# Latent attention's queries and keys made feature-major directly, with the rotation left to the score product

## The chip, the cores and the metric

The kernel runs on one core of one Trainium2 chip. The metric is the device time of one execution in microseconds (us); the number of a kernel is the median of its runs.

## The reference, cut to what matters

The model is a four-part encoder trunk (mixer, MLP, mixer, MLP) over 256 tokens of width 1024. The first mixer has two groups of heads side by side: eight heads of neighbourhood attention, and eight heads of latent attention, which the change touches. In these, queries come out of a normed latent of 256 features and keys and values out of a normed latent of 128; a query or key has 64 plain features and 32 that are rotated by position, and the 32 rotated key features are one vector shared by all heads.

```python
def apply_rope(x, cos, sin):
    ...
    x1, x2 = x[..., :half], x[..., half:]
    return jnp.concatenate([x1 * c - x2 * s, x2 * c + x1 * s], axis=-1)

def even_mixer(xn, w_in, rpb, q_norm, w_uq, kv_norm, w_ukv, w_o, cos_r, sin_r):
    hcat = xn @ w_in
    ...
    c_q = rms_norm(hcat[..., o0:o1], q_norm)
    c_kv = rms_norm(hcat[..., o1:o2], kv_norm)
    k_pe = apply_rope(hcat[..., o2:][:, :, None, :], cos_r, sin_r)
    q = (c_q @ w_uq).reshape(b, s, MLA_HEADS, MLA_NOPE + MLA_ROPE)
    q = jnp.concatenate([q[..., :MLA_NOPE], apply_rope(q[..., MLA_NOPE:], cos_r, sin_r)], axis=-1)
    kv = (c_kv @ w_ukv).reshape(b, s, MLA_HEADS, MLA_NOPE + MLA_V)
    k = jnp.concatenate([kv[..., :MLA_NOPE],
                         jnp.broadcast_to(k_pe, (b, s, MLA_HEADS, MLA_ROPE))], axis=-1)
    v = kv[..., MLA_NOPE:]
    out_b = dense_attention(q, k, v, (MLA_NOPE + MLA_ROPE) ** -0.5)
    return jnp.concatenate([out_a, out_b], axis=-1) @ w_o
```

## The kernel before

The program has four stages in a row: the even mixer, an MLP, the odd mixer, an MLP. Weights are read from HBM in pieces of up to 128 x 2048, four raw buffers deep, over SP's queue; each piece is split on ScalarE and VectorE into a high and a low fp32r half (`split`: a cast on ScalarE, line 175, and the remainder on VectorE, line 176; tiles `whi`, `wlo`), and a product is three matmuls, high by high, low by high and high by low (`mm3`, lines 179 to 181). The weights come in the order of a list (`plan`), and each call of `weight()` splits up to two pieces ahead.

In the even mixer the latents come first: `c_product` gives 416 columns a token (256 for queries, 128 for keys and values, 32 rotary), and `c_tail` (lines 511 to 531) norms them, rotates the 32 columns with four VectorE operations (`rope`, lines 494 to 498) into `kpe`, and hands back a step that turns the normed latent `cn` feature-major by three TensorE transposes (line 530) and splits it into `c`. There is one such step for each half `t` of the tokens; the two stand among the matmuls of the neighbourhood queries and keys. The first fills the time of `t` = 0 and the second that of `t` = 1.

Then `main` is a list of steps with costs in us, written by hand: the neighbourhood products, the latent queries (`uq_steps`) and keys and values (`ukv_steps`), and the output product (`out_steps`). `side` is the list of attention steps: for each n of 0 to 15, `scores(n)` (line 676; 0 to 7 neighbourhood, 8 to 15 latent, two heads and 128 tokens each), `turn_probs(n)` (transposes of the probabilities `pp`, line 709, copied to `pts`) and `mix` (line 724). A loop gives out as many side steps as the costs of the main steps have earned. The tile scheduler then fixes the order on each engine; an engine works through its queue strictly in that order.

A latent product is token-major: for each half `t` and four heads `h`, six matmuls of 384 columns give queries, ScalarE copies the plain features to `qtok`, VectorE rotates the others into it, and a later step `turn` makes four transposes of 128 x 96 (`heads_transposed`, line 615) and splits the outcome into `mq`. Keys and values are made together, three matmuls of 512 columns; ScalarE copies the keys to `ktok`, GpSimd copies `kpe` beside them (line 656), VectorE copies the values to `vml`, and four transposes and a split give `mk`. The scores contract over 96 features.

Of the kernel before, what the change touches and what calls it, by code (L numbers as in the profile page):

```python
# [23 lines left out]
P = 128  # L24
# [20 lines left out]
def trunk(ctx, tc, a, out):  # L45
# [37 lines left out]
    warm = const.tile([P, 512], mybir.dt.bfloat16, name="warm")  # L83
    nc.vector.memset(warm, 0.0)
    idle = bank("acc")
# [38 lines left out]
    plan("w_uq", 2 * 768)  # L124
# [346 lines left out]
    def even(ep):  # L471
# [30 lines left out]
        cT_h, cT_l = halves(quarter_pair("c"))  # L502
        kpe = ep.tile([P, NT, 32], F32, name="kpe")
# [7 lines left out]
        def c_tail(t, pc):  # L511
            rt = column(r, t)
            cn = scratch([384], "cn")
# [98 lines left out]
        def heads_transposed(n, t, h, src):  # L612
            pt = bank("w")
            for i in range(4):
                nc.tensor.transpose(pt[0:96, i * P:(i + 1) * P], src[:, i, :], ident)
            hs = slice(4 * h, 4 * h + 4)
            split(*(mT[n][0:96, hs, v, tok(t)] for v in range(2)), pt[0:96].rearrange("p (i n) -> p i n", i=4))

        def uq_steps():
            hold, src = {}, {}  # L620

            def gemm(t, h):
                if not hold:
                    hold["w"] = weight()
                    mT["q"] = pair_tile(ep, KT, "mq", 1, "mq")
                wh, wl = hold["w"]
                pq = bank("acc")
                for k in range(2):
                    ws = slice(k * 768 + h * 384, k * 768 + h * 384 + 384)
                    mm3(pq[:, 0:384], cT_h[:, k, tok(t)], cT_l[:, k, tok(t)], wh[:, ws], wl[:, ws], k == 0, k == 1)  # L630
                pq4 = pq[:, 0:384].rearrange("p (h d) -> p h d", d=96)
                s = src[t, h] = scratch([4, 96], "qtok")
                nc.scalar.copy(s[:, :, 0:64], pq4[:, :, 0:64])
                rope(s[:, :, 64:96], pq4[:, :, 64:96], 4, cosr[:, t, :], sinr[:, t, :], 16)

            def turn(t, h):
                heads_transposed("q", t, h, src.pop((t, h)))

            th = [(t, h) for t in range(NT) for h in range(2)]
            return [lambda v=v: gemm(*v) for v in th], [lambda v=v: turn(*v) for v in th]  # L640

        def ukv_steps():
            hold, src = {}, {}

            def gemm(t, h):
                if not hold:
                    hold["w"] = weight()
                    mT["k"] = pair_tile(ep, KT, "mk", 1, "mk")
                wh, wl = hold["w"]
                pk = bank("acc")  # L650
                ws = slice(h * 512, h * 512 + 512)
                mm3(pk, cT_h[:, 2, tok(t)], cT_l[:, 2, tok(t)], wh[:, ws], wl[:, ws], True, True)
                pk4 = pk.rearrange("p (h d) -> p h d", d=128)
                s = src[t, h] = scratch([4, 96], "ktok")
                nc.scalar.copy(s[:, :, 0:64], pk4[:, :, 0:64])
                nc.gpsimd.tensor_copy(s[:, :, 64:96], kpe[:, t, :].unsqueeze(1).broadcast_to([P, 4, 32]))
                nc.vector.tensor_copy(vml[:, t, h * 256:(h + 1) * 256].rearrange("p (h d) -> p h d", d=64), pk4[:, :, 64:128])

            def turn(t, h):
                heads_transposed("k", t, h, src.pop((t, h)))  # L660

            th = [(t, h) for t in range(NT) for h in range(2)]
            return [lambda v=v: gemm(*v) for v in th], [lambda v=v: turn(*v) for v in th]
# [12 lines left out]
        def scores(n):  # L676
# [7 lines left out]
            else:  # L684
                for j in range(2):
                    h = 2 * hp + j
                    q, k = (halves(mT[n][0:96, h]) for n in "qk")
# [55 lines left out]
        (ug, ut), (kg, kt) = uq_steps(), ukv_steps()  # L743
# [236 lines left out]
def _constants():  # L980
    con = {}
    con["cos_r"], con["sin_r"] = _tables(32, ORDER)
    con["cos_f"], con["sin_f"] = (np.ascontiguousarray(np.tile(z.transpose(1, 0, 2).reshape(T, HD).T, (2, 1)))
# [66 lines left out]
```

## Time and profile before

| | |
|---|---|
| median of 3 runs | 751.15 us (751.09 to 751.2) |
| the profiled execution | 751.89 us, of which 750.0 us span |
| PE (TensorE matmul) busy | 739.8 us, 99% |
| VectorE (DVE), ScalarE (ACT), GpSimd (POOL) busy | 542.3, 468.6, 9.5 us |
| share of TensorE in the chain that ended last | 93% |
| mean granted TensorE clock | 0.998 |

The span is the time from the first to the last instruction. The chain that ended last is followed back from the last instruction, at each step to what released it. A busy PE counts matmuls from their start to a modelled end, and neighbours overlap: the price of a matmul in a dense stretch is the distance between two starts, not the duration of one.

### The profile page before, as it was taken

The page shows a single profiled execution, that of the slowest core. Times are in us where ns is not written, and L with a number is a line of the kernel's source. Part 1 is how long each engine was busy: PE and PEld are TensorE (multiplying, and loading weights), DVE is VectorE, ACT ScalarE, POOL GpSimd, SP SyncE. Part 2 cuts the span into 40 slices and gives each one's busy share as a digit, 9 for nine tenths or more (in the row PEclk, how much of TensorE's full clock was granted, in tenths as well). Part 3 has the DMA queues.
Part 4 walks back from the last instruction along what each step waited for, and adds up shares of the span by engine and source line. Part 5 has one row for each costly group of instructions (what it writes and reads, how often), then busy time and mean ns, then how long its engine had stood idle before and what let it go on. Part 6 is the DMA issues. An engine that isn't in the chain of part 4 may idle for free.

```text
span 750.0 us, 12208 instructions
## 1 busy us (share of the span) xinstructions
PE 739.8 (99%) x4572; PEld 644.8 (86%) x4572; DVE 542.3 (72%) x1143; ACT 468.6 (62%) x1059; POOL 9.5 (1%) x22
## 2 busy tenths in 40 slices
PE   8999999999999999999999999999999999999996
PEld 5887899888888888989899898998998888888885
DVE  6798859766656656998877787877759665666664
ACT  6688887545545446857785866867757554554541
POOL 0100000000000000000000000000000000000000
PEclk9999999999999999999999999999999999999999
DMA  8854333655555554575656546556653555555501
GB/s 265 332 211 155 113 114 111 228 176 184 202 190 184 187 182 148 194 229 183 197 162 201 204 153 213 172 177 197 204 200 145 200 194 180 175 208 177 184 33 57
DMA packets 27419, 135.29 MB, mean 180 GB/s; under 512 B 4448, under 2 KB 7008, under 8 KB 14432
## 3 DMA queue, kind: packets, MB, share of 16 engines
q1 hardware_dynamic: 27072, 134.23, 52.6%
q8 instruction: 36, 0.59, 0.3%
q10 hardware_dynamic: 288, 0.28, 0.1%
q14 instruction: 23, 0.19, 0.1%
HBM read 127.16 MB, written 1.05 MB: 171 GB/s over the span
## 4 chain that ended last, share of the span: by engine, by line
PE 93%; DVE 2%; DMA 2%; issue 1%; ACT 1%; SPq 0%; POOLq 0%; POOL 0%; DVEq 0%
PE w L185 16%; PE acc L185 14%; PE acc L179 13%; PE acc L180 13%; PE acc L181 13%; PE w L186 8%; PE acc L186 7%; PE w L900 1%; PE w L200 1%; PE w L882 1%; DMA raw<-in_w_v 1%; PE acc L915 1%; PE w L709 1%; PE w L724 1%; DMA raw<-in_w_c 1%
## 5 line engine op out<-in xcount | busy, mean ns | idle before, releaser
L176 DVE TENSOR_TENSOR wlo<-raw,whi 128x512 fp32r<-128x512 f32 (+3 forms) x488 | 302.8, 661 | 70.5 <-ACT whi L175 70.0
L175 ACT CAST whi<-raw 128x512 fp32r<-128x512 f32 (+3 forms) x488 | 263.3, 602 | 81.9 <-issue 69.6
L185 PE MATMUL w<-xT,whi 128*128 128x512 f32 x528 | 185.1, 394 | 0.0
L185 PE MATMUL acc<-xT,whi 128*128 128x512 f32 x432 | 155.3, 402 | 0.0
L186 PE MATMUL w<-xT,wlo 128*128 128x256 f32 x528 | 137.0, 280 | 0.0
L185 PEld LDWEIGHTS w<-xT,whi 128*128 128x128 f32 x528 | 96.5, 187 | 18.8
L186 PE MATMUL acc<-xT,wlo 128*128 128x256 f32 x432 | 112.2, 280 | 0.0
L186 PEld LDWEIGHTS w<-xT,wlo 128*128 128x128 f32 x528 | 99.1, 188 | 5.7
L179 PE MATMUL acc<-whi,h 128*128 128x512 f32 x250 | 98.4, 393 | 0.0
L180 PE MATMUL acc<-wlo,h 128*128 128x512 f32 x250 | 97.8, 391 | 0.0
L181 PE MATMUL acc<-whi,h 128*128 128x512 f32 x250 | 97.4, 390 | 0.0
L185 PEld LDWEIGHTS acc<-xT,whi 128*128 128x128 f32 x432 | 78.8, 188 | 14.7
L186 PEld LDWEIGHTS acc<-xT,wlo 128*128 128x128 f32 x432 | 81.2, 188 | 4.1 <-issue 0.2
L192 ACT COPY up<-w 128x256 f32<-128x256 f32 x64 | 23.9, 373 | 88.5 <-PE w L185 88.5
L193 DVE TENSOR_TENSOR up<-up,w 128x256 f32<-128x256 f32 x64 | 26.8, 419 | 63.0 <-ACT up L192 62.3
L179 PE MATMUL acc<-whi,xT 128*128 128x384 f32 (+2 forms) x160 | 56.5, 353 | 1.0 <-ACT whi L175 0.9
L180 PE MATMUL acc<-wlo,xT 128*128 128x384 f32 (+2 forms) x160 | 56.0, 350 | 0.4 <-DVE wlo L176 0.4
L181 PEld LDWEIGHTS acc<-whi,h 128*128 128x128 f32 x250 | 47.0, 188 | 10.2
L180 PEld LDWEIGHTS acc<-wlo,h 128*128 128x128 f32 x250 | 47.0, 188 | 9.7
L181 PE MATMUL acc<-whi,xT 128*128 128x384 f32 (+2 forms) x160 | 55.3, 345 | 0.0
L179 PEld LDWEIGHTS acc<-whi,h 128*128 128x128 f32 x250 | 46.9, 188 | 9.1
L192 ACT COPY qk<-acc 128x256 f32<-128x256 f32 x48 | 17.0, 370 | 30.0 <-PE acc L185 29.4
(186 smaller groups left out, 965.2 us busy)
## 6 DMA issues: line engine op xcount, KB each, us to landing
raw<-in_w SPq DMA_DIRECT2D x64, 1024.0 KB, 4.8
raw<-in_w_oqk SPq DMA_DIRECT2D x24, 1024.0 KB, 5.0
raw<-in_w_ov SPq DMA_DIRECT2D x16, 768.0 KB, 4.7
sw<-qk SPq DMA_DIRECT2D x96, 64.0 KB, 2.6
raw<-in_w_qk SPq DMA_DIRECT2D x4, 1024.0 KB, 10.5
raw<-in_w_oe SPq DMA_DIRECT2D x4, 1024.0 KB, 4.9
raw<-in_w_oo SPq DMA_DIRECT2D x4, 1024.0 KB, 5.3
bias<-in_rpb SPq DMA_DIRECT2D x8, 256.0 KB, 4.4
```

What stands on the lines that cost most here:

```text
L175: a = nc.scalar.copy(hi, src).ins
L176: return a, (eng or nc.vector).tensor_tensor(lo, src, hi.bitcast(F32), op=ALU.subtract).ins
L179: nc.tensor.matmul(o, sh, mh, start=first, stop=False)
L180: nc.tensor.matmul(o, sh, ml, start=False, stop=False)
L181: nc.tensor.matmul(o, sl, mh, start=False, stop=last)
L185: both = lambda: nc.tensor.matmul(o, sh, m.rearrange("p v n -> p (v n)"), start=first, stop=last)
L186: low = lambda: nc.tensor.matmul(o[:, 0:T], sl, m[:, 0, :], start=False, stop=False)
L192: nc.scalar.copy(dst, o[:, T:2 * T])
L193: nc.vector.tensor_tensor(dst, dst, o[:, 0:T], op=ALU.add)
L200: nc.tensor.matmul(o[j], qk[pb, 0, a, ts], qk[pb, 1, b, :], start=n == 0, stop=n == 2)
L709: nc.tensor.transpose(pt[:, b * P:(b + 1) * P], pp[:, b // 2, (b % 2) * P:(b % 2 + 1) * P], ident)
L724: nc.tensor.matmul(pvo[64 * j:64 * j + 64, tok(t)], v[:, kk, h * 64:(h + 1) * 64], pts[:, 2 * j + kk, :], start=kk == 0, stop=kk == NT - 1)
```

## The change

The query weights are laid out on the host with 128 columns a head in place of 96: the 64 plain ones, the 32 rotary ones, and the same 32 with their halves exchanged. For odd heads the plain ones come last. The product is made feature-major at once: the weights are stationary, the latent `c` is the moving side with 256 tokens, and one step `m` gives two heads in one bank of 2 x 256. On its way out of PSUM the bank is multiplied by a table `turns` (128 x 2 x 256: ones at the plain features, cosines at the rotary ones, sines at the exchanged ones) and split into `mq`. The keys' plain features are made likewise, and their other 64 rows hold the rotated shared key twice; so the contraction over 128 rows adds plain, cosine and sine parts, and the rotation of the queries is summed by the scores.

For that, `c_tail` rotates the key into four equal copies of 32 columns that become columns 384 to 512 of `cn`; the latent is turned by four transposes in place of three, and `c` gets a fourth chunk. GpSimd copies rows of this chunk into `mk` for four heads at a time, two copies of 64 x 2048. Values are a product of their own, token-major, 512 columns. The transposes of `qtok` and `ktok` and the copies to them are gone. The table is a new load of 256 KB ahead of the norm gains; `w_uq` grows from 128 x 1536 to 128 x 2048.

```diff
     plan("w_ukv", 1024)
-    plan("w_uq", 2 * 768)
+    plan("w_uq", WCH)
...
             nc.sync.dma_start(sinr, a["sin_r"])
+            nc.sync.dma_start(turns, a["turns"])
             nc.sync.dma_start(gc[:, 0:256], a["q_norm"].partition_broadcast(P))
...
-            cn = scratch([384], "cn")
+            cn = scratch([512], "cn")
...
-            rope(kpe[:, t, :].unsqueeze(1), kp.unsqueeze(1), 1, cosr[:, t, :], sinr[:, t, :], 16)
+            rope(cn[:, 384:512].rearrange("p (n w) -> p n w", w=32), kp.unsqueeze(1).broadcast_to([P, 4, 32]), 4,
+                 cosr[:, t, :], sinr[:, t, :], 16)

             def step():
                 pt = bank("w")
-                for k in range(3):
+                for k in range(4):
                     nc.tensor.transpose(pt[:, k * P:(k + 1) * P], cn[:, k * P:(k + 1) * P], ident)
-                split(cT_h[:, 0:3, tok(t)], cT_l[:, 0:3, tok(t)], pt[:, 0:384].rearrange("p (k n) -> p k n", k=3))
+                split(cT_h[:, :, tok(t)], cT_l[:, :, tok(t)], pt.rearrange("p (k n) -> p k n", k=4))
...
+        def query_steps():
+            hold = {}
+
+            def step(m):
                 if not hold:
...
+                    hold["w"] = latent_weight("q", "mq")
                 wh, wl = hold["w"]
...
+                pq = two(bank("acc"))
+                for j in range(2):
+                    for k in range(2):
+                        c = slice(k * D + (2 * m + j) * P, k * D + (2 * m + j + 1) * P)
+                        mm3(pq[:, j], wh[:, c], wl[:, c], cT_h[:, k], cT_l[:, k], k == 0, k == 1)
+                q32 = scratch([2, T], "qm")
+                nc.vector.tensor_tensor(q32, pq, turns, op=ALU.mult)
+                split(*halves(mT["q"][:, 2 * m:2 * m + 2]), q32)
+
+            return [lambda m=m: step(m) for m in range(4)]
+
+        def key_value_steps():
+            hold = {}
+
+            def keys(b):
                 if not hold:
...
+                    hold["w"] = latent_weight("k", "mk")
+                    for j, rows in enumerate((slice(64, P), slice(0, 64))):
+                        nc.gpsimd.tensor_copy(by_parity(mT["k"])[rows, j], cT[rows, 3].unsqueeze(1).broadcast_to([64, 4, 2, T]))
                 wh, wl = hold["w"]
...
+                pk = two(bank("acc"))
+                for m in range(2):
+                    c = slice((2 * b + m) * P, (2 * b + m + 1) * P)
+                    mm3(pk[:, m], wh[:, c], wl[:, c], cT_h[:, 2], cT_l[:, 2], True, True)
+                for j, rows in enumerate((slice(0, 64), slice(64, P))):
+                    o = by_parity(mT["k"])[rows, j, 2 * b:2 * b + 2]
+                    split(o[:, :, 0], o[:, :, 1], pk[rows])
+
+            def values(t):
+                wh, wl = hold["w"]
+                pv = bank("acc")
+                mm3(pv, cT_h[:, 2, tok(t)], cT_l[:, 2, tok(t)], wh[:, 512:D], wl[:, 512:D], True, True)
+                nc.any.tensor_copy(out=vml[:, t], in_=pv)
...
-        i = lambda t, h: 2 * t + h
-        for h in range(2):
-            main += [(.65, kg[i(0, h)]), (.98, ug[i(0, h)]), (.43, kt[i(0, h)]), (.65, kg[i(1, h)]), (.43, ut[i(0, h)]),
-                     (.98, ug[i(1, h)]), (.43, kt[i(1, h)]), (.43, ut[i(1, h)])]
+        for i, (c, f) in enumerate(zip((.72, .72, .68, .68), kg)):
+            main += [(c, f), (1.43, ug[i])]
```

The order of instructions moves in three places. On VectorE, in the latents' tail of the second half of the tokens (`t` = 1), the kernel before has this piece; `kp` is the scaled rotary columns, `r_369` and `r_370` are the two products of the rotation, `q_403` neighbourhood queries and keys, `wlo` the remainder of a weight piece:

```order
L522 SCALAR_TENSOR_TENSOR cn<-acc,rstd,gc 128x128
L524 TENSOR_SCALAR kp<-acc,rstd 128x32
L494 TENSOR_TENSOR r_369<-kp,cosr 128x32
L496 TENSOR_TENSOR r_370<-kp,sinr 128x16 x2
L176 TENSOR_TENSOR c<-w,c 128x3x128
L498 TENSOR_TENSOR kpe<-r_369,r_370 128x32
```

The changed kernel has this in the same place (its line numbers are one to four higher), down to the split of the second half of the latent:

```order
L527 TENSOR_SCALAR kp<-acc,rstd 128x32
L496 TENSOR_TENSOR r_370<-kp,cosr 128x128
L498 TENSOR_TENSOR r_371<-kp,sinr 128x4x16 x2
L177 TENSOR_TENSOR wlo<-raw,whi 128x512
L500 TENSOR_TENSOR cn<-r_370,r_371 128x128
L194 TENSOR_TENSOR q_404<-q_404,w 128x256 x2
L177 TENSOR_TENSOR c<-w,c 128x4x128
L607 TENSOR_TENSOR q_404<-q_404,both 128x512
L177 TENSOR_TENSOR wlo<-raw,whi 128x512 x2
L177 TENSOR_TENSOR qk<-q_404,qk 128x2x256
L177 TENSOR_TENSOR wlo<-raw,whi 128x512
L177 TENSOR_TENSOR c<-w,c 128x4x128
```

The rotation's sum, which nobody on TensorE waited for while it went to `kpe`, is now the last part of `cn`, and a weight remainder stands between its products and its sum.

On GpSimd, between the powers of the latents' norms (line 218) and the clearing of two tiles of the odd mixer, the kernel before has the first row, and the changed one the second:

```order
L656 COPY ktok<-kpe 128x4x32 x4
```

```order
L649 COPY mk<-c 64x4x512 x2
```

Each copy reads `c` alone and so stands ready as soon as the second half of the latent is split.

On TensorE, around the scores of n = 5 (`qk`, the second row of this piece), the kernel before has the latent products in groups with the transposes of `ktok` and `qtok` between them:

```order
L724 MATMUL acc<-pts,vna 64x128 x8
L200 MATMUL w<-qk 128x256 x6
L615 MATMUL w<-ident,ktok 96x128 x4
L709 MATMUL w<-ident,pp 128x128 x4
L179 MATMUL acc<-whi,c 128x512
L180 MATMUL acc<-wlo,c 128x512
L181 MATMUL acc<-whi,c 128x512
L179 MATMUL acc<-whi,c 128x384
L180 MATMUL acc<-wlo,c 128x384
```

The changed kernel has the latent products with the weights stationary, the transposes of `pp` alone between them, and the scores of n = 6 at the end of this piece:

```order
L711 MATMUL w<-ident,pp 128x128 x4
L180 MATMUL acc<-c,whi 128x256
L181 MATMUL acc<-c,whi 128x256
L182 MATMUL acc<-c,wlo 128x256
L180 MATMUL acc<-c,whi 128x256
L181 MATMUL acc<-c,whi 128x256
L182 MATMUL acc<-c,wlo 128x256
L201 MATMUL w<-qk 128x256 x6
```

The transposes of `ktok` and `qtok` are gone from the queue, and the scores of n = 6 follow those of n = 5 with fewer instructions between them.

## Rows read from the trace of the kernel before

**Rows 1.** Busy time of each engine (instructions), by stretch; clock, DMA share, GB/s.

```profile
core 0: us, PE busy (x) PEld busy (x) DVE busy (x) ACT busy (x) POOL busy (x), PEclk, DMA share, GB/s
34.00:60.00 26.00, 26.00 (x176) 21.64 (x176) 23.30 (x70) 21.52 (x62) 1.14 (x3) 1.00 0.64 227
60.00:90.00 30.00, 28.62 (x230) 24.05 (x230) 26.00 (x81) 26.41 (x72) 0.61 (x3) 1.00 0.36 126
```

**Rows 2.** Waits of TensorE, whole span: us, times, longest.

```profile
PE acc L179 <- DVE oa L176: 0.7, 1, 0.7
...
PE w L615 <- DVE mn L694: 0.5, 1, 0.5
```

**Rows 3.** TensorE in order of time: start, duration, line, operation.

```profile
60.05 0.34 PE L179 MATMUL acc<-whi,c 128*128 128x384 f32 x1
...
60.92 0.34 PE L181 MATMUL acc<-whi,c 128*128 128x384 f32 x1
...
66.06 0.61 PE L615 MATMUL w<-ident,qtok 128*96 128x128 f32 x4 [0.46 <-DVE mn L694]
66.60 0.93 PE L200 MATMUL w<-qk 64*128 64x256 f32 x6
...
77.05 0.28 PE L179 MATMUL w<-mk,mq 96*128 96x256 f32 x1
...
78.25 0.28 PE L180 MATMUL acc<-oa,whi 128*128 128x256 f32 x1
...
85.06 0.60 PE L615 MATMUL w<-ident,qtok 128*96 128x128 f32 x4
85.50 0.60 PE L709 MATMUL w<-ident,pp 128*128 128x128 f32 x4
```

**Rows 4.** VectorE in order of time, the tail of the latents and a rotation of queries.

```profile
34.46 1.28 DVE L176 TENSOR_TENSOR wlo<-raw,whi 128x512 fp32r<-128x512 f32 x2
...
36.93 0.24 DVE L524 TENSOR_SCALAR kp<-acc,rstd 128x32 f32<-128x32 f32 x1
...
64.50 0.28 DVE L494 TENSOR_TENSOR r<-acc,cosr 128x128 f32<-128x128 f32 x1
64.70 0.34 DVE L496 TENSOR_TENSOR r<-acc,sinr 128x64 f32<-128x64 f32 x2
```

**Rows 5.** TensorE in order of time, the transposes of the latent for t = 1.

```profile
37.09 0.49 PE L530 MATMUL w<-ident,cn 128*128 128x128 f32 x3
```

**Rows 6.** GpSimd by line and shape: busy us, mean ns, idle before.

```profile
L790 POOL MEMSET k<- 128x1024 f32 x2 | 1.8, 958 | 225.3 <-PE acc L181 225.3
...
L656 POOL COPY ktok<-kpe 128x128 f32<-128x128 f32 x4 | 1.2, 300 | 35.1 <-ACT pp L699 30.1 <-PE w L615 5.1
```

**Rows 7.** GpSimd in order of time.

```profile
30.87 0.92 POOL L218 TENSOR_TENSOR rstd<-ss,mhalf 128x1 f32<-128x1 f32 x1 [2.97 <-DVE ss L519]
33.29 0.54 POOL L218 TENSOR_TENSOR rstd<-ss,mhalf 128x1 f32<-128x1 f32 x1 [1.50 <-DVE ss L519]
...
72.45 0.30 POOL L656 COPY ktok<-kpe 128x128 f32<-128x128 f32 x1 [5.05 <-PE w L615]
```

**Rows 8.** VectorE in order of time, beside rows 7 and after the latents.

```profile
30.71 0.68 DVE L176 TENSOR_TENSOR wlo<-raw,whi 128x512 fp32r<-128x512 f32 x1
...
43.45 0.41 DVE L694 CUSTOM_DVE_ANT_0 sn<-w,bias 128x256 f32<-128x256 f32 x1
43.80 0.08 DVE L694 DVE_READ_ACCUMULATOR2_ANT mn<- 128x1 f32 x1
43.80 0.68 DVE L603 TENSOR_TENSOR q<-q,both 128x512 f32<-128x512 f32 x1
...
72.57 0.71 DVE L176 TENSOR_TENSOR wlo<-raw,whi 128x512 fp32r<-128x512 f32 x1 [0.96 <-ACT whi L175]
```

**Rows 9.** ScalarE in order of time, the probabilities of n = 0.

```profile
46.14 0.91 ACT L702 ACTIVATE pp<-pp,rz 128x256 f32<-128x256 f32 x2 [0.24 <-DVE rz L700]
```

**Rows 10.** TensorE in order of time, the transposes of these probabilities.

```profile
47.25 0.66 PE L709 MATMUL w<-ident,pp 128*128 128x128 f32 x4
```

More of the change, by code (lines that the diff above doesn't have):

```diff
@@ L80, in trunk @@
     x = act.tile([P, KT, T], F32, name="x")
-    warm = const.tile([P, 512], mybir.dt.bfloat16, name="warm")
+    warm = scratch([256], "warm")
     nc.vector.memset(warm, 0.0)
+    warm = warm.bitcast(mybir.dt.bfloat16)
     idle = bank("acc")
@@ L498, in rope @@
             nc.vector.tensor_tensor(dst, t1, t2, op=ALU.add)
-        cT_h, cT_l = halves(quarter_pair("c"))
-        kpe = ep.tile([P, NT, 32], F32, name="kpe")
+        cT = quarter_pair("c")
+        cT_h, cT_l = halves(cT)
+        turns = ep.tile([P, 2, T], F32, name="turns")
         vna = ep.tile([P, NT, 512], F32, name="vna")
@@ L610, in even, with by_parity @@
         mT = {}
[L612 to L622, printed above, removed]
+        def by_parity(z):
+            return z.rearrange("p (m j) v n -> p j m v n", j=2)
@@ L623, in gemm, with latent_weight @@
+        def latent_weight(nm, name):
+            mT[nm] = pair_tile(ep, KT, name, 1, name)
+            return weight()
+        def query_steps():
+            hold = {}
+            def step(m):
                 if not hold:
-                    hold["w"] = weight()
-                    mT["q"] = pair_tile(ep, KT, "mq", 1, "mq")
+                    hold["w"] = latent_weight("q", "mq")
                 wh, wl = hold["w"]
[L627 to L640, printed above, removed]
@@ L649, in gemm @@
                 wh, wl = hold["w"]
[L650 to L663, printed above, removed]
+                pk = two(bank("acc"))
+                for m in range(2):
+                    c = slice((2 * b + m) * P, (2 * b + m + 1) * P)
+                    mm3(pk[:, m], wh[:, c], wl[:, c], cT_h[:, 2], cT_l[:, 2], True, True)
@@ new lines, in keys @@
+                for j, rows in enumerate((slice(0, 64), slice(64, P))):
[6 more added lines that the diff above has]
+                nc.any.tensor_copy(out=vml[:, t], in_=pv)
+            return [lambda b=b: keys(b) for b in range(2)] + [lambda t=t: values(t) for t in range(NT)]
@@ L686, in scores @@
                     h = 2 * hp + j
-                    q, k = (halves(mT[n][0:96, h]) for n in "qk")
+                    q, k = (halves(mT[n][:, h]) for n in "qk")
                     mm3(sb[:, j], q[0][:, tok(t)], q[1][:, tok(t)], *k, True, True)
@@ L741, in attention @@
             return out
-        (ug, ut), (kg, kt) = uq_steps(), ukv_steps()
+        ug, kg = query_steps(), key_value_steps()
         first = qk_steps(0)
@@ L982, in _constants @@
     con["cos_r"], con["sin_r"] = _tables(32, ORDER)
+    c, s = (z.transpose(1, 0, 2).reshape(T, 32).T for z in (con["cos_r"], con["sin_r"]))
+    one = np.ones((64, T), np.float32)
+    con["turns"] = np.ascontiguousarray(np.stack([np.concatenate([one, c, s]), np.concatenate([c, s, one])], 1))
     con["cos_f"], con["sin_f"] = (np.ascontiguousarray(np.tile(z.transpose(1, 0, 2).reshape(T, HD).T, (2, 1)))
@@ L1002, in _layout @@
     d["w_v"] = f(w[:, 1024:1536].reshape(2, 4, P, 512).transpose(0, 2, 1, 3).reshape(2, P, -1))
-    d["w_uq"] = f(i["ev_w_uq"][0].reshape(1, 2, P, 768).transpose(0, 2, 1, 3).reshape(1, P, -1))
-    d["w_ukv"] = f(i["ev_w_ukv"][0].reshape(1, P, 1024))
+    uq, ukv = i["ev_w_uq"][0].reshape(256, 8, 96), i["ev_w_ukv"][0].reshape(P, 8, 2, 64)
+    nope, turn = uq[..., :64], np.concatenate([uq[..., 64:], np.roll(uq[..., 64:], 16, -1)], -1)
+    uq = np.stack([np.concatenate([nope, turn], -1)[:, 0::2], np.concatenate([turn, nope], -1)[:, 1::2]], 2)
+    d["w_uq"] = f(uq.reshape(1, 2, P, D).transpose(0, 2, 1, 3).reshape(1, P, -1))
+    d["w_ukv"] = f(ukv.transpose(0, 2, 1, 3).reshape(1, P, 1024))
     d["w_oe"] = f(i["ev_w_o"][0].reshape(4, 2, P, D).transpose(0, 2, 1, 3).reshape(4, P, -1))
```

5 lines of the change are left out of this document (removed).

## The prediction

> **What bounds the kernel now.** I read the table of engines first, then the busy times by stretch, then TensorE's own waits, and last the order of time on each engine around the change. TensorE is the bound: 739.8 of 750.0 us busy at full clock, and 93% of the chain that ended last. In the stretch from 34 to 60 us it never idles, while VectorE is busy for 23.3 of 26 us. From 60 to 90, where the latent queries and keys are made, TensorE has 28.62 of 30 and VectorE and ScalarE some 26 each [rows 1]. So every TensorE instruction taken out of 34 to 90 is worth its slot, unless a wait takes the slot. There are only 1.4 us of waits in 60 to 90; the two longest are for VectorE, 0.7 for the remainder of a mix that frees a bank and 0.5 in front of a transposition of `qtok` [rows 2]. Behind 90 us nothing is changed and TensorE stays full, so what is won or lost here reaches the end of the kernel; DMA engines are at 0.36 in this stretch and no wait of TensorE names one.
>
> **The change, part by part.** *TensorE's slots.* In a dense stretch six matmuls of 384 columns start 0.87 us apart from first to last, so 0.174 each; eleven of 256 columns start within 1.20 us, so 0.120 each, whatever tile is stationary [rows 3]. Queries: 24 x 0.174 = 4.18 become 48 x 0.120 = 5.76, which costs 1.58. Keys and values: twelve of 512 columns become twelve of 256 and six of 512. By the slope between the two prices a 512 takes 0.228, so six of them, 1.37, become twelve of 256, 1.44: plus 0.07. Removed are eight groups of four transposes, sixteen for queries and sixteen for keys. A group holds the queue for 0.44 us (85.06 to 85.50), and for 0.54 at the worst (66.06 to 66.60) [rows 3]; at 0.48 that is 3.84 (3.5 to 4.3). Added are two transposes of the latent at a quarter of 0.44: 0.22. The score matmuls keep 256 columns; that they contract over 128 rows and not 96 changes no column count. Sum: 1.58 + 0.07 + 0.22 - 3.84 = **-2.0 us** (-2.4 to -1.6).
>
> *A new wait at the latent's transposes.* The rotated key was nobody's hurry; now it is the last quarter of `cn`. For t = 1, `kp` starts at 36.93 and takes 0.24; the wide products start 0.20 apart and the pair of sine products takes 0.34, the weight remainder that the order puts between takes 0.64, half of the pair in the rows, and the sum 0.28 like the wide product [rows 4]. That ends at 38.6. The two remainders that stood at 34.46 are no longer in this piece of the queue, while the same tail for t = 0 is wider by some 0.4; the chain through GpSimd's powers stays. I put the end 0.25 earlier, at 38.35. TensorE reaches these transposes at 37.09 [rows 5]; with one more for t = 0 and three before the fourth, its turn comes at 37.09 + 4 x 0.11 = 37.53. Behind it in the strict queue stand the neighbourhood matmuls, so TensorE idles: **+0.9 us** (0.3 if the queue in front empties sooner, 1.3 if it does not at all).
>
> *GpSimd's copies.* Two copies of 64 x 2048 replace four of 128 x 128. Before shows no such copy. Below, a clearing of 1024 columns takes 0.958, so 2048 take 1.9 us; above, 0.30 for 128 columns, taken wholly per column, gives 4.8 [rows 6]. I take 2 us each, since the short copy must hold a start-up cost as the clearing does. They run from about 43.4 us, when the second half of `c` is split, and the first latent scores that read them come more than 25 us later, so their own time is covered at either bound. What they may cost is VectorE's time beside them. A power on GpSimd took 0.92 us when a VectorE remainder with both inputs in SBUF had started 0.16 us before it, and 0.54 without [rows 7, 8]: GpSimd waited for VectorE. In the other direction a copy began at 72.45 and took 0.30, and a remainder begun at 72.57 took 0.71 against 0.68 elsewhere [rows 7, 8]: little to be seen, but the copy is short. The Trainium skill (SBUF — State Buffer, section on the two separate sides) says that a VectorE instruction with two SBUF inputs and a GpSimd instruction that reads SBUF exclude each other for a whole instruction. The 0.92 us agrees with that; the 0.71 neither proves nor refutes it.
>
> If VectorE waits, the first to be late is the product of `q` with `both`, at 43.80 before [rows 8] and about 44.2 now. Behind it stand the second score reduction of n = 0, a remainder, a split and the reciprocal, and for these ScalarE's probabilities, done at 47.05 [rows 9], and TensorE's transposes at 47.25 [rows 10]. TensorE comes 1.1 us later than before (0.9 + 0.22) and VectorE some 0.45, so the slack of 0.2 grows to 0.85. One copy that holds VectorE from 43.4 to 45.4 makes it 1.2 late and TensorE 0.35. I take **+0.4 us** (0 without any exclusion; the upper end is a rival below).
>
> *Waits in 60 to 77.* The scores, probabilities and copies between n = 5 and n = 8 stay. VectorE gives up the rotations and value copies of [rows 4]'s kind, and gets a table product and remainder for each pair of heads and narrower key remainders: about the same time. ScalarE loses eight short copies, but not the eight casts. TensorE asks for the same work in 2 us less. Two of the waits go with the transposes, others come at the transposes of `pp`: I leave the sum at 1.4 us, **0** (from -1.4 to +1.0).
>
> *Covered.* The table is one more SP issue and 256 KB ahead of the gains, `w_uq` another 256 KB; the engines are at 0.64 and 0.36 in the two stretches [rows 1] and no transfer ends a TensorE wait there. Where that cover is missing, SP's later loads of `w_qk` come up to 1 us later, ahead of which VectorE and ScalarE have whole pieces split already. The wider split of `c` and the larger `w_uq` cost VectorE and ScalarE half a us each before 60, where VectorE has 2.7 us idle.
>
> Sum: -2.0 + 0.9 + 0.4 + 0 = -0.7 us. The profiled execution took 751.89, 0.74 above the median; the difference is set against the median: 751.15 - 0.7 = **750.4 us**.
>
> **The rivals.** *Faster.* The waits of 60 to 77 go: both of [rows 2] end with instructions that the change removes or moves, and there are fewer handovers between engines. With no cost from GpSimd: -2.0 + 0.9 - 1.4 = -2.5, 748.6 us. Against it: VectorE and ScalarE are 87% busy there and lose little.
>
> *TensorE's slots turn into waits.* If softmax on ScalarE and VectorE sets the pace from n = 5 on, the 2 us won come back as waits: -2.0 + 0.9 + 0.4 + 2.0 = +1.3, 752.4 us. For it: the busy shares [rows 1]. Against it: splits of later weights stand between and have slack after 90.
>
> *Slower.* The two GpSimd copies run one after the other, hold the port for 2.5 us each, and VectorE does not get in between: from 43.4 to 48.4, which makes the `both` product 4.2 late and TensorE 4.2 - 0.85 = 3.3. Then -2.0 + 0.9 + 3.3 = +2.2, 753.3 us. It decides when both hold VectorE for more than 4.2 us together. This is the exclusion in the Trainium skill named above, taken at its word. Against it: the 0.71 at 72.57, and that copies of different partitions may overlap.
>
> **How the numbers follow.** The forecast (750.4) has 0.37, the faster case (748.6) 0.35, waits for slots (752.4) 0.12, the port (753.3) 0.16. About 0.2%, 1.5 us, is what a measurement of this kernel can tell from no change. The first and third cases lie within it: same 0.49; faster 0.35; slower 0.16. The range from 748.4 to 752.6 holds the first three and leaves out most of the fourth and the tail of the second. The likeliest case's own range, by the bounds of its terms, is 749.4 to 751.6.
>
> **What would show it.** Right: no rows of `qtok` and `ktok`, 48 matmuls of 256 columns 0.12 apart; an idle time of about 0.9 us before a transposition of `cn` near 38 us, released by VectorE; GpSimd copies of about 2 us from 43 on; idle time of TensorE in 60 to 77 near 1.4. Wrong: no idle time at 38, or VectorE rows with two SBUF inputs stretched by whole microseconds beside the copies, or more than 2.5 us of TensorE idle between n = 5 and n = 8. The prediction fails low if both waits vanish, and high if the copies shut VectorE out.

## The result, and the profile after

The changed kernel takes 752.24 us (median; 751.65 to 752.94) beside 751.16 us for the kernel before, measured together: a ratio of 1.0013, 95% interval 1.0007 to 1.0019. It is slower by 1.1 us, where -0.7 was forecast. The time lies in the range, but on the other side of no change. The profiled execution took 752.55 us with a span of 750.7.

The busy times by stretch, the rows that answer to [rows 1]:

```profile
core 0: us, PE busy (x) PEld busy (x) DVE busy (x) ACT busy (x) POOL busy (x), PEclk, DMA share, GB/s
34.00:60.00 26.00, 24.19 (x162) 19.14 (x160) 24.48 (x64) 21.32 (x59) 4.74 (x4) 1.00 0.56 199
60.00:90.00 30.00, 29.33 (x243) 25.07 (x239) 26.95 (x71) 26.99 (x72) 0.00 (x0) 1.00 0.36 125
```

TensorE, which never idled between 34 and 60 us, now idles for 1.8 us there, while between 60 and 90 it idles for 0.7 us less than before. VectorE is busy for 1.2 us more in the first stretch with six instructions fewer, so its instructions have become longer on average, and GpSimd is busy for 4.74 us where it had 1.14.

TensorE's waits between 34 and 60 and between 60 and 90, which answer to [rows 2] (total, times, longest):

```profile
PE w L711 <- ACT pp L704: 0.9, 1, 0.9
PE w L534 <- DVE cn L500: 0.9, 1, 0.9
...
PE w L711 <- ACT pp L704: 0.4, 1, 0.4
PE acc L726 <- ACT pts L713: 0.2, 1, 0.2
```

The two waits of [rows 2] are gone, and four others are there. Four engines in order of time show where the two near 38 and 49 us come from. These rows answer to [rows 4], [rows 5] and [rows 7] to [rows 10]:

```profile
37.32 0.68 DVE L177 TENSOR_TENSOR wlo<-raw,whi 128x512 fp32r<-128x512 f32 x1
37.92 0.28 DVE L500 TENSOR_TENSOR cn<-r,r 128x128 f32<-128x128 f32 x1
...
38.26 0.33 PE L534 MATMUL w<-ident,cn 128*128 128x128 f32 x1 [0.87 <-DVE cn L500]
...
43.24 4.20 POOL L649 CAST mk<-c 64x2048 fp32r<-64x2048 f32 x2 [7.17 <-ACT q L193]
...
44.00 1.68 DVE L607 TENSOR_TENSOR q<-q,both 128x512 f32<-128x512 f32 x1
45.61 0.41 DVE L696 CUSTOM_DVE_ANT_0 sn<-w,bias 128x256 f32<-128x256 f32 x1
...
45.95 2.04 DVE L177 TENSOR_TENSOR wlo<-raw,whi 128x512 fp32r<-128x512 f32 x1
...
48.70 0.91 ACT L704 ACTIVATE pp<-pp,rz 128x256 f32<-128x256 f32 x2 [1.60 <-DVE rz L702]
...
49.26 0.84 PE L711 MATMUL w<-ident,pp 128*128 128x128 f32 x4 [0.94 <-ACT pp L704]
```

At 38 us the rotated key's sum comes out behind a weight remainder, and TensorE stands for 0.87 us in front of the fourth transposition, as forecast. At 43.24 the two GpSimd copies begin. The product of `q` with `both`, 0.68 us in [rows 8], takes 1.68; the remainder after it takes 2.04. The score reduction between them, which has only one input in SBUF, keeps its 0.41. Together the two rows are 2.36 us longer, the reciprocal comes that much later, ScalarE waits 1.60 us for it, and TensorE 0.94 us for ScalarE.

A ledger from the start times of TensorE's rows says the rest. I take the stretch from the first matmul of `w` on `xT` (29.29 us before, 29.00 after) to the same matmul in the next block (118.44 and 119.22), and give each instruction the time from its start to the next start, less the idle time that the row names. "Of the change" are the projections from the latent and the transpositions of `cn`, `qtok` and `ktok`.

| us | before | after | copies by DMA | and later transposes |
|---|---|---|---|---|
| stretch | 89.15 | 90.22 | 88.24 | 87.93 |
| named waits | 1.38 | 2.45 | 1.20 | 0.64 |
| slots of the change | 12.19 | 10.79 | 10.75 | 10.56 |
| all other slots | 75.58 | 76.98 | 76.29 | 76.73 |

The last two columns are experiments told below (e1_dma and e3_both). The change does take 1.40 us of slots away; waits bring 1.07 back, and another 1.40 sits in all the other instructions. In sum +1.07, close to the 1.1 of the medians. That it is so close is partly luck: the ledger is one execution of each kernel, and these two as a whole differ by 0.66 us (751.89 and 752.55), since the changed one came to the stretch 0.29 earlier and took some 0.1 less behind it.

### The profile page after: what moved, and what is told of

The parts are those of the page before. It is cut to its first block, busy times and chain, and to the rows that moved or that the text cites. A ratio compares the mean times of both kernels' runs of the same rounds, so it can differ in the third digit from the quotient of the medians.

```text
span 750.7 us, 12178 instructions
## 1 busy us (share of the span) xinstructions
PE 739.7 (99%) x4572; PEld 644.4 (86%) x4572; DVE 547.0 (73%) x1130; ACT 466.5 (62%) x1050; POOL 12.0 (2%) x20
## 4 chain that ended last, share of the span: by engine, by line
PE 88%; DVE 4%; ACT 3%; DMA 2%; issue 2%; SPq 1%; POOL 0%; POOLq 0%; DVEq 0%; ACTq 0%
PE w L186 16%; PE acc L180 13%; PE acc L182 13%; PE acc L181 13%; PE acc L186 12%; PE w L187 8%; PE acc L187 6%; DVE wlo L177 2%; PE w L900 1%; DMA raw<-in_w_v 1%; PE w L882 1%; PE w L201 1%; PE acc L915 1%; PE w L726 1%; PE w L711 1%
```

## The experiments

The theory behind them: the copies on GpSimd and VectorE instructions with two SBUF inputs shut each other out, which costs some 1.7 us, and the late rotated key costs another 0.9 or so. The rival: VectorE has more work, or work in a worse order, and is late whoever copies. All comparisons are with the kernel before on the same chip, whose median was 751.4 to 751.7 us.

**e1_dma: the copies by DMA.**

```diff
...
-nc.gpsimd.tensor_copy(by_parity(mT["k"])[rows, j], cT[rows, 3].unsqueeze(1).broadcast_to([64, 4, 2, T]))
+nc.sync.dma_start(by_parity(mT["k"])[rows, j].bitcast(F32), cT[rows, 3].unsqueeze(1).broadcast_to([64, 4, 2, T]).bitcast(F32))
```

> The changed kernel with the two GpSimd copies of the rotated key made by DMA from the SP queue; everything else stays. Theory (GpSimd copies shut VectorE's two-input instructions out): the product of q with both near 44 us and the weight remainder near 46 us take 0.68 us each again instead of 1.68 and 2.04, the idle time of 0.94 before the first transposes of pp (n = 0) falls below 0.2, and the kernel takes 752.2 - 1.7 = 750.5 us (ratio to before 0.9991; 0.9987 to 0.9997). Rival (VectorE and ScalarE have more or differently ordered work there and are late whoever copies): the rows are short again, but the wait at pp stays above 0.7, and the time stays at 752.2 (1.0013). Third possibility: the copies at the SP queue's head hold back the loads of bias and weights behind them, with a wait for a DMA and 753 or more.

Measured: 751.03 us, ratio 0.9995 (0.9986 to 1.0003). Its VectorE and TensorE rows in order of time:

```profile
44.12 0.68 DVE L607 TENSOR_TENSOR q<-q,both 128x512 f32<-128x512 f32 x1
...
45.07 0.69 DVE L177 TENSOR_TENSOR wlo<-raw,whi 128x512 fp32r<-128x512 f32 x1
...
48.39 0.66 PE L711 MATMUL w<-ident,pp 128*128 128x128 f32 x4
```

VectorE's order is the same and the row lengths are back, so the rival falls: the lateness belongs to the copies. TensorE no longer waits for the probabilities of n = 0. The time fell by 1.2 us against the changed kernel (1.4 by the two ratios to before), less than the 1.7 expected, though the interval reaches there.

**e2_later: the second latent transposes one piece later.**

```diff
-        main.insert(1, (0, turn_c[1]))
+        main.insert(2, (0, turn_c[1]))
```

> The changed kernel with the second half of the latent's transposes asked for one piece of query and key projections later (1.3 us of TensorE work), copies on GpSimd as in the changed kernel. Theory (the rotated key comes late for a TensorE that stands there at 36.9 us): the idle time of 0.87 before the fourth transposition of cn goes to 0, and everything up to n = 0's scores comes 0.9 to 1.1 earlier; the copies start up to 0.5 later and still stretch two VectorE rows, so the wait at pp stays at 0.6 to 1.5. Time 752.2 - 1.0 = 751.2 us (ratio 1.0000; 0.9995 to 1.0008). Rival (TensorE is paced by VectorE in this stretch, so that a wait removed in one place comes back at the next): 752.2 (1.0013), with the 0.9 found again before the transposes of pp.

Measured: 753.56 us, ratio 1.0023 (1.0014 to 1.0033): no gain, and if anything a loss. TensorE's and VectorE's rows:

```profile
38.87 0.60 PE L534 MATMUL w<-ident,cn 128*128 128x128 f32 x4
...
44.40 2.01 DVE L607 TENSOR_TENSOR q<-q,both 128x512 f32<-128x512 f32 x1
...
46.68 2.03 DVE L177 TENSOR_TENSOR wlo<-raw,whi 128x512 fp32r<-128x512 f32 x1
...
49.98 0.84 PE L711 MATMUL w<-ident,pp 128*128 128x128 f32 x4 [2.18 <-ACT pp L704]
```

The wait at `cn` is gone, as the theory said, and comes back before the probabilities, 2.18 instead of 0.94, as the rival said. The two costs are not independent: as long as the copies hold VectorE back, an earlier TensorE only waits longer. The time is above both expected ones, and that part is not explained: the ledger's stretch is 90.42 us, 0.2 more than in the changed kernel, and this execution came to it 0.56 later (29.56), ahead of the edit.

**e3_both: both edits.** The two diffs above together.

> Both edits together: the copies by DMA and the second latent transposes one piece later. Theory (two separate costs that add): neither wait is there, 752.2 - 1.7 - 1.0 = 749.5 us (ratio 0.9978; 0.9972 to 0.9987), which is the slots of 2 us won in full. Rival (one of the waits only covers for the other): the time is that of the better of the two edits alone, 750.5 or more.

Measured: 750.05 us, ratio 0.9980 (0.9971 to 0.9989). This beats both kernels, by 1.4 us against before. Between 34 and 60 us no wait of TensorE is left. With the copies gone the later transposes do pay: 1.0 us by the medians of e1_dma and e3_both, as expected. The ledger shows only 0.31 of it, because the wait at `cn` happened to be 0.53 in the profiled execution of e1_dma; it is 0.88 to 0.90 in e4_memset, e8_one, e9_late and e12_costs_alone, which leave these transposes where they were.

**e4_memset: GpSimd writes the same region without reading it.**

```diff
+mark_t = ep.tile([P, 2, 32], F32R, name="mark")
...
+mark = nc.gpsimd.tensor_copy(mark_t[rows, j], cT[rows, 3, 0, 0:32]).ins
+with tc.issue_after(mark):
-    nc.gpsimd.tensor_copy(by_parity(mT["k"])[rows, j], cT[rows, 3].unsqueeze(1).broadcast_to([64, 4, 2, T]))
+    nc.gpsimd.memset(by_parity(mT["k"])[rows, j].bitcast(F32), 0.0)
```

> The changed kernel with each GpSimd copy of 64 x 2048 replaced by a GpSimd clearing of the same region at the same place (a copy of 64 x 32 from the latent ahead of each holds it back until the latent is there); the shared rotated key is left out of the scores by this, which changes no instruction elsewhere. Theory (what shuts VectorE out is GpSimd reading SBUF): the clearings take 1.5 to 2 us each from about 43.4 us, the VectorE rows beside them take 0.68 us, the wait at pp is below 0.2, time 750.5 us (ratio 0.9991). Rival (any GpSimd instruction, or its writing, shuts them out): VectorE rows stretched to 1.7 and 2.0 as before, wait at pp 0.9, time 752.2 (1.0013).

Measured: 751.09 us, ratio 0.9995 (0.9986 to 1.0004). The clearings ran earlier than meant, since the small copies needed only the first half of the latent, but they ran beside VectorE rows of the kind in question. GpSimd and VectorE in order of time:

```profile
37.91 1.81 POOL L652 MEMSET mk<- 64x2048 f32 x1
39.92 1.80 POOL L652 MEMSET mk<- 64x2048 f32 x1
...
38.11 0.68 DVE L177 TENSOR_TENSOR wlo<-raw,whi 128x512 fp32r<-128x512 f32 x1
...
40.18 0.67 DVE L607 TENSOR_TENSOR q<-q,both 128x512 f32<-128x512 f32 x1
40.78 1.28 DVE L177 TENSOR_TENSOR wlo<-raw,whi 128x512 fp32r<-128x512 f32 x2
```

Two instructions of 1.8 us that write 64 x 2048 stretch nothing, no wait comes before the first probabilities, and the time is that of e1_dma. So it is not the writing that shuts VectorE out, which leaves the reading. The Trainium skill says the same (SBUF — State Buffer, section "Who interferes with whom"): two SBUF inputs contend with a GpSimd instruction that reads SBUF, not with one that only writes it. The rows here agree.

**e6_before_copies: the suspected cost alone, in the kernel before.**

```diff
...
+        def copies():
+            mT["k"] = pair_tile(ep, KT, "mk", 1, "mk")
+            by_parity = mT["k"].rearrange("p (m j) v n -> p j m v n", j=2)
+            for j, rows in enumerate((slice(64, P), slice(0, 64))):
+                nc.gpsimd.tensor_copy(by_parity[rows, j], cT[rows, 2].unsqueeze(1).broadcast_to([64, 4, 2, T]))
+
         main.insert(1, (0, turn_c[1]))
+        main.insert(2, (0, copies))
```

> The kernel before with nothing of the change but two GpSimd copies of 64 x 2048, taken from the latent's third quarter when its second half is split, into the key tile, whose rows are written again later. Theory (GpSimd's copies shut out VectorE's two-input instructions, and the probabilities of n = 0 come late by it): copies of 2.1 us each from about 41.3 us, two or three VectorE rows of 0.68 stretched by 2.0 to 2.7 in sum, a new wait of 1.4 to 2.4 before the transposes of pp (n = 0), where before had none, and 751.2 + 2.0 = 753.2 us (ratio 1.0027; 1.0018 to 1.0036). Rival (the loss belongs to the change's other VectorE work and order, and an otherwise idle GpSimd costs nothing): no stretched rows, 751.2 us (1.0000).

Measured: 755.73 us, ratio 1.0048 (1.0036 to 1.0061), twice the expected loss. GpSimd, VectorE and TensorE:

```profile
40.95 4.53 POOL L762 CAST mk<-c 64x2048 fp32r<-64x2048 f32 x2 [4.77 <-DVE c L176]
...
41.67 4.36 DVE L176 TENSOR_TENSOR wlo<-raw,whi 128x512 fp32r<-128x512 f32 x2
...
49.52 1.11 PE L709 MATMUL w<-ident,pp 128*128 128x128 f32 x4 [2.41 <-ACT pp L702]
```

Two remainders take 4.36 us instead of 1.28, so 3.1 are lost on VectorE, above the 2.0 to 2.7 expected, and 2.41 on TensorE. The remaining 1.6 us of the stretch (93.15 against 89.15 in the ledger's measure) goes by TensorE's clock. Three stretches of 1 us: busy time (instructions) of each engine, the granted clock, DMA share, GB/s:

```profile
48.00:49.00 1.00, 0.00 (x0) 0.00 (x0) 1.00 (x4) 0.75 (x4) 0.00 (x0) 1.00 0.39 55
...
50.00:51.00 1.00, 1.00 (x5) 0.90 (x5) 1.00 (x5) 0.11 (x1) 0.00 (x0) 0.50 0.99 115
...
53.00:54.00 1.00, 1.00 (x9) 0.79 (x9) 0.46 (x2) 0.87 (x3) 0.00 (x0) 1.00 0.94 389
```

After the wait the clock is granted at 0.72 from 49 to 50 us, at 0.50, which is 1.2 GHz, from 50 to 52, at 0.57 up to 53, and in full from then on; at 0.50 TensorE starts five matmuls per us, at 1.00 nine. What is missing from full speed in these four stretches, 0.28 + 0.50 + 0.50 + 0.43, makes 1.7 us. So the theory holds with its mechanism and its price for the wait, and the expectation missed what the wait sets off. One of the five executions, of which there is no trace, shows a mean clock of 0.999 where the other four have 0.995 to 0.997, and took 753.61 us, close to the 753.2 expected.

**e7_pieces: the same bytes in eight pieces.**

```diff
-                        nc.gpsimd.tensor_copy(by_parity(mT["k"])[rows, j], cT[rows, 3].unsqueeze(1).broadcast_to([64, 4, 2, T]))
+                        for m in range(4):
+                            nc.gpsimd.tensor_copy(by_parity(mT["k"])[rows, j, m], cT[rows, 3])
```

> The changed kernel with each of the two GpSimd copies cut into four of 64 x 512, same bytes, same place. Theory (the exclusion is held for one instruction at a time): VectorE gets in between pieces, so that no two-input row waits for more than one piece of about 0.55 us; the rows at 44.0 and 46.0 are stretched by 1.0 to 1.5 in sum instead of 2.4, the wait at pp is 0.3 or less, and the time is 752.2 - 0.9 = 751.3 us (ratio 1.0002; 0.9995 to 1.0008). Rival (pieces follow one another without a gap that VectorE could use): the sum of the stretch stays 2 or more and the time 752.2 (1.0013).

Measured: 752.39 us, ratio 1.0009 (1.0000 to 1.0018): not told apart from the changed kernel. The rows:

```profile
43.49 7.27 POOL L650 CAST mk<-c 64x512 fp32r<-64x512 f32 x8 [7.17 <-ACT q L193]
...
44.24 0.96 DVE L607 TENSOR_TENSOR q<-q,both 128x512 f32<-128x512 f32 x1
...
46.14 1.10 DVE L177 TENSOR_TENSOR qk<-q,qk 128x512 fp32r<-128x512 f32 x1
...
47.23 3.05 DVE L177 TENSOR_TENSOR wlo<-raw,whi 128x512 fp32r<-128x512 f32 x3
...
48.51 0.66 PE L712 MATMUL w<-ident,pp 128*128 128x128 f32 x4
...
53.29 0.84 PE L712 MATMUL w<-ident,pp 128*128 128x128 f32 x4
```

The theory had the mechanism right: no row waits for more than one piece, and the wait before the first probabilities is gone. But the eight pieces take 7.27 us instead of 4.20, because GpSimd now waits in turn, and three remainders that stood behind the copies in the changed kernel take 3.05 instead of 1.87. With these, five rows are stretched by 1.9 us in sum, nearly the rival's 2, and the rival's time came. TensorE gets from n = 0 to n = 1 in 4.78 us (48.51 to 53.29) where e1_dma needs 4.06 (48.39 to 52.45). The loss is spread out and pushed to the next head.

**e8_one: one copy on GpSimd, one by DMA.**

```diff
-                    for j, rows in enumerate((slice(64, P), slice(0, 64))):
-                        nc.gpsimd.tensor_copy(by_parity(mT["k"])[rows, j], cT[rows, 3].unsqueeze(1).broadcast_to([64, 4, 2, T]))
+                    shared = lambda j, rows: (by_parity(mT["k"])[rows, j], cT[rows, 3].unsqueeze(1).broadcast_to([64, 4, 2, T]))
+                    nc.gpsimd.tensor_copy(*shared(0, slice(64, P)))
+                    nc.sync.dma_start(*(z.bitcast(F32) for z in shared(1, slice(0, 64))))
```

> The changed kernel with one of the two copies left on GpSimd and the other made by DMA. Theory (TensorE had 1.4 us of room at pp: 2.4 of stretched rows made a wait of 0.94): only the row at 44.0 is stretched, by 1.0, the first wait at pp goes wholly, and the time is that without any GpSimd copy, 751.0 to 751.2 us (ratio 0.9996; 0.9989 to 1.0004). Rival (each copy costs its share): 751.6 and a wait of 0.4 to 0.5 at pp.

Measured: 751.38 us, ratio 0.9996 (0.9987 to 1.0005). GpSimd, VectorE and TensorE:

```profile
43.03 1.90 POOL L649 CAST mk<-c 64x2048 fp32r<-64x2048 f32 x1 [7.17 <-ACT q L193]
...
43.79 1.69 DVE L607 TENSOR_TENSOR q<-q,both 128x512 f32<-128x512 f32 x1
...
45.74 0.68 DVE L177 TENSOR_TENSOR wlo<-raw,whi 128x512 fp32r<-128x512 f32 x1
...
48.05 0.66 PE L712 MATMUL w<-ident,pp 128*128 128x128 f32 x4
```

One copy (1.90 us by itself) makes VectorE 1.0 us late, and no wait at the first probabilities follows. The theory's number came; 751.6 of the rival lies in the interval too, so the row decides and not the time.

**e9_late: both copies later, on GpSimd.** They are held back by a small copy of the first keys' low part; the two copies at the earlier place are taken out.

```diff
...
+                if b == 0:
+                    mark_t = ep.tile([64, 32], F32R, name="mark")
+                    mark = nc.gpsimd.tensor_copy(mark_t, by_parity(mT["k"])[0:64, 0, 0, 1, 0:32]).ins
+                    with tc.issue_after(mark):
+                        for j, rows in enumerate((slice(64, P), slice(0, 64))):
+                            nc.gpsimd.tensor_copy(by_parity(mT["k"])[rows, j], cT[rows, 3].unsqueeze(1).broadcast_to([64, 4, 2, T]))
```

> The changed kernel with both GpSimd copies held back until the first keys are split (near 66 us, by a copy of 64 x 32 from them that stands ahead). Theory (a GpSimd copy costs what VectorE's slack at its place does not take up): the waits at pp of n = 0 go, the rows of VectorE with two SBUF inputs near 66 to 71 are stretched by 2 to 3 in sum, and the wait at pp of n = 5, 0.43 near 70 us, grows to 1.5 to 2.5, since VectorE is 88% busy there: 752.2 - 1.2 + 1.4 = 752.4 us (ratio 1.0015; 1.0006 to 1.0025). Rival (only the place at 43 us is short of slack): the waits of 60 to 90 stay at 0.6, 751.0 us (0.9996).

Measured: 753.70 us, ratio 1.0030 (1.0017 to 1.0043). VectorE and TensorE:

```profile
64.00 2.14 DVE L177 TENSOR_TENSOR qk<-q,qk 128x512 fp32r<-128x512 f32 x1
...
66.20 0.50 PE L201 MATMUL w<-qk 64*128 64x256 f32 x4 [0.40 <-DVE qk L177]
...
69.72 0.84 PE L715 MATMUL w<-ident,pp 128*128 128x128 f32 x4 [1.39 <-ACT pp L708]
```

The cost moved with the copies and did not shrink: 0.40 at the scores and 1.39 instead of 0.43 at the probabilities of n = 5, where 1.5 to 2.5 was expected. The profiled stretch of the ledger is 90.15 us, as long as in the changed kernel (90.22), so the theory's reading of the profile holds; this execution took 752.72 us. The median is 1.3 us above the expected 752.4: the longest execution took 755.53 with a mean clock of 0.994, and no trace shows where that clock was lost.

**e10_pool_queue: both edits, the DMA asked for from GpSimd's queue.** Against e3_both:

```diff
...
-nc.sync.dma_start(
+nc.gpsimd.dma_start(
...
```

> Both edits (copies by DMA, second latent transposes one piece later), the DMA asked for from GpSimd's queue, where nothing stands behind it, instead of SP's, where the loads of the score biases stand behind it. Theory (issuing a DMA from GpSimd reads no SBUF for long, so VectorE isn't shut out, and the bias comes in time): VectorE's wait of 0.31 for a bias near 51 us goes, TensorE's waits stay at 0.64 in all, and the time is that of the version with SP's queue or 0.2 less, 749.9 us (ratio to before 0.9979; 0.9971 to 0.9988). Rival (writing the transfers' descriptors on GpSimd takes the port or comes late): VectorE rows near 44 to 50 above 0.68 and a wait at pp, 751 or more.

Measured: 756.13 us, ratio 1.0057 (1.0041 to 1.0072). Neither theory nor rival: the rows from 44 to 50 are short, and something else is late. VectorE and TensorE:

```profile
55.24 0.42 DVE L696 CUSTOM_DVE_ANT_0 sn<-w,bias 128x256 f32<-128x256 f32 x1 [4.58 <-DMA bias<-in_rpb]
...
57.88 1.12 PE L726 MATMUL acc<-pts,vna 128*64 128x128 f32 x8 [4.08 <-DVE pts L713]
```

Issues of DMA between 40 and 62 us, with size and median time to landing; then the loads of the bias between 30 and 62 us, first here and then in e3_both; then a stretch behind the wait, with the granted clock as the third number from the end:

```profile
mk<-c POOLq DMA_DIRECT2D x2, 512.0 KB, 9.2
bias<-in_rpb SPq DMA_DIRECT2D x4, 256.0 KB, 6.8
...
DMA to landing us min/median/max: 2.7/6.8/10.2
...
DMA to landing us min/median/max: 4.2/5.1/6.0
...
58.00:60.00 2.00, 2.00 (x15) 1.44 (x15) 1.44 (x5) 1.80 (x5) 0.00 (x0) 0.50 0.82 328
```

With SP's queue the copies stand between the loads: a bias lands in 4.2 to 6.0 us in e3_both. From GpSimd's queue both copies (1 MB) go out at once at 44 us, SP's queue lets a weight load of 1 MB follow at 48, and the bias asked for at 44.87 takes until 55. By these rows the queue that I took for a hindrance was the spacing; no run separates that from the change of queue itself. As in e6_before_copies the wait is not the whole price: the clock is granted at 0.50 from 58 to 64 us, and the stretch of the ledger is 6.8 us longer than in e3_both, of which 4.1 are waits and 2.7 other slots.

**e11_costs and e12_costs_alone: the planner's costs by the measured slots,** once with both edits and once without. Only the costs are shown.

```diff
-        for i, (c, f) in enumerate(zip((.72, .72, .68, .68), kg)):
-            main += [(c, f), (1.43, ug[i])]
+        for i, (c, f) in enumerate(zip((.85, .85, .85, .85), kg)):
+            main += [(c, f), (1.63, ug[i])]
```

> Both edits, and the costs by which the planner mixes attention into the projections set to the slots that the trace shows (0.85 for a piece of keys or values and 1.63 for one of queries, where 0.70 and 1.43 stand). Theory (the slots that the change saves are fewer than predicted because 256-column matmuls cost 0.136 and not 0.120 in this mixture, whatever the order): 748.5 to 751.5, no difference from the version with both edits alone (ratio 0.998; 0.997 to 0.999), and TensorE's 60 matmuls of 256 columns on the latent still hold 8.2 us. Rival (attention steps come too early by the wrong costs and lose time at the borders): the stretch to the first matmul of the next block is 0.5 to 1 us shorter, 749.3 us (0.997).

> The changed kernel with nothing but the planner's costs set to the slots that the trace shows (0.85 and 1.63); the copies stay on GpSimd, the second latent transposes where they were. Theory (the costs only thin out the attention steps, which takes the wait of n = 5 near 70 us away, 0.43; the VectorE rows stretched by the copies and the waits at cn and at the pp of n = 0 are ahead of that and stay): 752.2 - 0.5 = 751.7 us (ratio 1.0006; 0.9998 to 1.0014). Rival (with the costs right, the other waits find room by themselves): the waits of 0.87 and 0.94 shrink below half, and the time is 750.5 or less (0.9990).

Measured: 749.43 us, ratio 0.9974 (0.9965 to 0.9983) with both edits; 751.68 us, ratio 1.0003 (0.9994 to 1.0012) alone. Alone, the waits of 0.87 and 0.9 stay and that of n = 5 goes, as its theory said. With both edits one wait is left between 34 and 90 us:

```profile
PE acc L726 <- ACT pts L713: 0.2, 1, 0.2
```

The rival of e11_costs came nearer: the stretch is 87.05 us, 0.88 less than in e3_both, of which 0.43 are the wait at n = 5, 0.10 slots of the change and 0.35 other slots. The 60 matmuls of 256 columns hold 8.06 us; the theory was right that they do not come near 60 x 0.120 = 7.2. The ratio's interval overlaps that of e3_both (0.9971 to 0.9989), so the rows decide here too. This is the best version found, 2.0 us under the kernel before.

## Why the prediction was wrong

**GpSimd's copies: this step failed.** The prediction had the mechanism, the place and the row that would be late, but took **+0.4 us**, "one copy that holds VectorE from 43.4 to 45.4". Both copies held it, one row each: the sign of being wrong that the prediction itself named, rows stretched by whole microseconds. By e1_dma the copies cost 0.94 in the wait at the first probabilities and 0.69 in other slots (76.98 to 76.29 in the ledger), together 1.6 us; the medians say 1.2. That is four times the term, or three, and enough by itself to turn the forecast gain into a loss. The reasoning against it was the 0.71 us at 72.57 in [rows 8], beside a copy of 0.30. That copy ended 0.18 us after the remainder had begun, so it could not show more than a trifle. And it did show it: the remainder ended 0.53 us after the copy (73.28 and 72.75). In the changed kernel the stretched rows end just as long after the copies, 0.54 us behind the first (45.68 and, by its 1.90 us, 45.14) and 0.55 behind the second (47.99 and 47.44). The row was held up like the others and agreed with the exclusion. The 0.92 us of a GpSimd power beside a remainder in [rows 7] was the better witness: a whole instruction waited for the other. The second half of the argument, that copies on different partitions may overlap, also fell: two take 4.20 us, one 1.90.

The "slower" rival described this course and put 3.3 us on it, with both copies holding VectorE without a break. VectorE does get in between: each copy costs one row, and the row that slips in delays the second copy.

**TensorE's slots: right in sign, too large by 0.6.** -2.0 was taken; the ledger shows -1.40, or -1.63 with the transposes moved. The 0.120 of [rows 3] holds inside a run. In the program runs are four to twelve long and other work stands between them. TensorE in e3_both:

```profile
62.10 0.39 PE L180 MATMUL acc<-c,whi 128*128 128x256 f32 x1
62.33 0.28 PE L181 MATMUL acc<-c,whi 128*128 128x256 f32 x1
...
63.53 0.28 PE L182 MATMUL acc<-c,wlo 128*128 128x256 f32 x1
63.65 0.60 PE L711 MATMUL w<-ident,pp 128*128 128x128 f32 x4
```

The first of this run holds 0.23 and the others 0.12. Over the stretch a matmul of 256 columns holds 0.136 (60 in 8.16 us), one of 384 held 0.200 before and not 0.174 (24 in 4.80). So the price of a matmul was too low on both sides, and that nearly cancels: all projections from the latent went from 8.11 to 9.86 us, +1.75 where +1.65 was forecast. Most of the 0.6 lies in the transposes: the removed ones were 3.59 us and not 3.84, and those of the latent grew by 0.44 and not 0.22 (by 0.22 in e3_both, where TensorE does not wait among them).

**The wait at the latent's transposes: right.** 0.9 was forecast, 0.87 came, released by the sum that the prediction named, at 38.2 instead of 38.35, behind the remainder that it named. The prediction's own two times, 38.35 and 37.53, are 0.82 apart; TensorE and the sum both came some 0.15 earlier.

**Waits in 60 to 77: 0 was forecast, -0.7 came** (0.64 instead of 1.38). Both waits of [rows 2] went, as the "faster" rival said, and 0.43 and 0.21 came at `pp` and `pts`. That is within the bounds of -1.4 and +1.0.

**What no step held:** all other slots grew by 1.40; the prediction left them at nothing without a reason. 0.69 of it goes with the copies by e1_dma. The rest, at least 0.7 us, stays in every version (0.71 in e1_dma, 0.80 in e11_costs, 1.15 in e3_both, against 75.58 before), so the division is known to some 0.4 us only; the ledger shows the rest spread over scores, neighbourhood projections and value mixes. That the borders between shorter runs cost it fits the rows above, but no run here separated it, and it stays open.

In sum: -0.7, +1.2 for the copies, +0.6 for slots of the change, +0.7 for other slots, -0.7 for the waits in 60 to 77 gives +1.1, the measured 1.1. The rival in which slots turn into waits lies nearest to the measured time with its 752.4, but that is luck: the waits from n = 5 on, which it wanted 2 us longer, became shorter. The covered edits (table, wider `w_uq`, wider split) show no wait of TensorE for a DMA between 34 and 90 us and cost nothing that can be seen.

## What to carry to other kernels

Before work is given to an idle GpSimd, count the VectorE instructions with two SBUF inputs that will run beside it: each GpSimd instruction that reads SBUF can hold up one of them for its whole length, and it is VectorE's next reader who pays. A short neighbour's length is weak evidence on a long one: look for a row in the trace where the suspected partner could have waited long, or compare when the row ends with when its neighbour ends. And when two waits lie on one path, undo them together before judging either: the later transposes alone won nothing, and with the copies on DMA they won.

## What the runs showed of the hardware

GpSimd copies 64 x 2048 values from SBUF to SBUF in 1.90 us, and two of them on different halves of the partitions run one after the other (4.20 us with a VectorE row in between). Beside them VectorE's two-input rows go from 0.68 to 1.68 and 2.04 us, rows with one SBUF input stay at 0.41, and two GpSimd clearings of the same size stretch nothing. A wait of 2.41 us in e6_before_copies was followed by some 3 us with TensorE's clock at or near half, which cost 1.6 us on top, and one of 4.08 us in e10_pool_queue by 6 us at half: a stall has a second price where the clock falls behind it. Behind the 2.18 us in e2_later it stayed at 1.00. And two DMA copies of 512 KB from SBUF to SBUF, asked for at once and followed by a weight load, kept a bias of 256 KB on its way for 10 us.
